# Sigmoid gates ahead of the latent attention, half of them parked in DRAM, and one output tile of the first branch per head

## The chip, the cores and the metric

The kernel runs on one core of a Trainium2 chip. The metric is device time in microseconds (us), from runs of the whole program; a profile is one more execution, recorded by the hardware. TensorE (PE) does the matrix products, with its weight loads as a row of their own (PEld); VectorE (DVE), ScalarE (ACT) and GpSimd (POOL) do the rest; SyncE (SP) issues the DMAs.

## The reference, cut to what matters

Two transformer blocks on 512 positions of width 1024, in float32. The change lies in the first half of the first block:

```
h = rms_norm(x, pre_mix_norm)
h_q, h_k, h_v, h_g, h_a, c_q, c_kv, k_pe = split(h @ w_in)
y_a = gla_branch(h_q, h_k, h_v, h_g, h_a, ...) @ w_o_gla          # first branch
y_b = mla_branch(c_q, c_kv, k_pe, cos, sin, ...) @ w_o_mla        # latent attention, 8 heads
g_a, g_b = split(sigmoid(h @ w_gate + b_gate))
mixed = (g_a * y_a + g_b * y_b) @ w_out
```

The latent attention normalises c_q and c_kv, makes from them the queries and keys of eight heads (128 columns without position and 64 with rope), and for blocks of 128 queries computes a masked softmax over the keys and its product with the values.

## The kernel before

**Layout.** Activations lie transposed: a tile has 128 features on the partitions and the 512 positions along the free side, so h is 8 tiles, the gates are 16 tiles (0 to 7 for the first branch, 8 to 15 for the second), and every output of width 1024 is 8 tiles. Each float32 operand is split into a high and a low part in a format that TensorE takes at full rate (`hi_lo`, line 129: ScalarE's cast at L135, VectorE's difference at L139 or L141). A product is three matmuls per step, high x high, low x high and high x low (`mm3`, line 205).

**A dense tile.** `lin` (line 212) makes one output tile of 128 x 512: it takes one of the PSUM banks of the ring `mm`, loads 512 KB of weights by one DMA on SP (`wload`, L179) into one of three raw buffers, splits them (two halves, L135 and L139), and runs 8 steps of 3 matmuls. `evac` (line 459) evicts the bank times the norm's factor R (L462 or L464). A gate is such a tile with a tanh after it (`gate`, lines 793 to 796); the sigmoid is written as half of one plus that tanh.

**Memory.** SBUF is cut by hand into 84 slots of 128 x 512 and 14 half slots; `A(name)` takes the slot that has been free longest and `free` puts it back at the end. A tile whose slot is still in use waits for it.

**Order.** The program is written as one long sequence, and a scheduler at build time fixes each engine's order: at each moment of a simulated timeline it takes, on every engine, the instruction earliest in the program among those whose inputs, slot and bank are ready. On the chip each engine then runs its list in that order, and so does SP with its DMAs. A DMA waits on SP for its buffer and its source. So later work can be placed ahead in gaps, but only as the simulated timeline saw them.

**The stages around the change.**

1. The first norm (lines 621 to 642). For the 8 tiles of x: the pair of x times the gain (ScalarE and VectorE), the weights of the first two output tiles, and their matmuls. Then, for each x, its square (ScalarE, L348) and the sum over the tiles (VectorE, L361). `hold2` holds two instructions behind which the squares and the sums are kept: here the last pair made. The sums give R through a small product (L375), a power on GpSimd (L332) and transposes (L383).
2. The first branch: its keys, values and queries, the scan over chunks in two halves of two heads (`gla_scan`), and its gated outputs (`gla_out`). The 8 tiles of its result (pairs, 16 slots) are `ogs`.
3. Lines 798 to 805. For n = 0 to 7: gate n, then output tile n of the first branch (`w_o_gla`), then `mix[n]` = (tanh + 1) x tile (L802). Then gates 8 to 11.
4. The latent attention's first inputs (lines 906 to 913): norms of c_q and c_kv, `mla_pair(0)` (rope queries of two heads and their values: rope copies on ScalarE at L613 and L614, two rows stacked by DMA at L851) and `mla_qk(0)`, `mla_qk(1)` (query and key of one head).
5. The loop over heads (lines 915 to 928). Head hd: its scores and softmax (`mla_scores`, L815 to L820, L887, L888), then the values of the head before it (`mla_values`, with transposes at L829), then the rope pair of heads hd + 2 and hd + 3 for even hd, and the query and key of head hd + 2. In heads 4 to 7 one more gate each, 12 to 15. After the last gate h and R are freed.
6. Lines 948 to 955. For n = 0 to 7: output tile n of the second branch (`w_o_mla`), times gate 8 + n, plus `mix[n]`. Then x is loaded again and the block goes on with `w_out`.

Of the kernel before, what the change touches and what calls it, by code (L numbers as in the profile page):

```python
# [10 lines left out]
F32 = mybir.dt.float32  # L11
# [3 lines left out]
ALU = mybir.AluOpType  # L15
AX = mybir.AxisListType

P = 128
T = 512
NT = T // P  # L20
DM = 1024
KD = DM // P
# [36 lines left out]
def two_blocks(ctx: ExitStack, tc: tile.TileContext, d, dbg=None):  # L59
    nc = tc.nc  # L60
    V, S, G, PE = nc.vector, nc.scalar, nc.gpsimd, nc.tensor

    NSLOT, NHALF = 84, 14
    cst = ctx.enter_context(tc.tile_pool(name="cst", bufs=1))
    ar = ctx.enter_context(tc.tile_pool(name="ar", bufs=1))
    pp = ctx.enter_context(tc.tile_pool(name="pp", bufs=1, space=bass.MemoryType.PSUM))


# [6 lines left out]
    def A(name, dt=F32, cols=T):  # L75
        if cols > 256 or len(spare_half) < 3:
            i = spare.popleft()
            low[0] = min(low[0], len(spare))
            ap = ar.tile([P, T], dt, tag="slot%d" % i, name=name)[:, :cols]
            owner[id(ap)] = (spare, i, ap, name)  # L80
        else:
            i = spare_half.popleft()
            ap = ar.tile([P, 256], dt, tag="half%d" % i, name=name)[:, :cols]
            owner[id(ap)] = (spare_half, i, ap, name)
        return ap

    def free(*xs):
        for x in xs:
            if isinstance(x, (tuple, list)):
                free(*x)  # L90
            else:
                home, i = owner.pop(id(x))[:2]
                home.append(i)
# [13 lines left out]
    def share(**kw):  # L107

        for name, which in kw.items():
            rings[name] = deque(which)  # L110

    def bank(name):
        i = rings[name].popleft()
        rings[name].append(i)
        return banks[i]

    MM, AT, OP, ST = (lambda: bank("mm")), (lambda: bank("at")), (lambda: bank("op")), (lambda: bank("st"))
# [26 lines left out]
    made, hold, hold2 = [], [], []  # L144
# [3 lines left out]
    def pair(name, src, scale=None, cols=T, eh=None, el=None):  # L148
        hi, lo = A(name + "h", F32R, cols), A(name + "l", F32R, cols)
        made[:] = hi_lo(hi[:, :cols], lo[:, :cols], src, scale, eh, el)  # L150
        return hi, lo
# [7 lines left out]
    def order(later, earlier):  # L159
        tc.add_manual_dep(later, earlier.name,  # L160
                          mybir.DependencyInfo(mybir.DependencyClass.NoSync, mybir.DependencyReason.DATA),
                          reason="table of functions")
# [27 lines left out]
    def wtile(w, n, kt, k0=0):  # L190

        step = 8
        ws = []
        for c0 in range(0, kt, step):
            ws.append(wload(w[n, :, (k0 + c0) * P:(k0 + min(kt, c0 + step)) * P]))
        return step, ws

    def wpart(wt, k):

        step, ws = wt  # L200
        hi, lo = ws[k // step][k % step // 4]
        s = slice(k % step % 4 * P, (k % step % 4 + 1) * P)
        return hi[:, s], lo[:, s]

    def mm3(ps, a, b, first, last):
        (ah, al), (bh, bl) = a, b
        r = PE.matmul(ps, lhsT=ah, rhs=bh, start=first, stop=False)  # L207
        PE.matmul(ps, lhsT=ah, rhs=bl, start=False, stop=False)  # L208
        PE.matmul(ps, lhsT=al, rhs=bh, start=False, stop=last)  # L209
        return r.ins  # L210

    def lin(w, n, hs, cols=T, k0=0, after=None):

        kt = len(hs)
        ps = MM()
        wt = wtile(w, n, kt, k0)
        for k in range(kt):
            r = mm3(ps[:, :cols], wpart(wt, k), hs[k], k == 0, k == kt - 1)
            if k == 0 and after:
                order(r, after)  # L220
        free(wt[1])
        return ps
# [178 lines left out]
    xs = [A("x") for k in range(KD)]  # L401
# [27 lines left out]
    def vcol(name, i=0, n=1):  # L429
        return vec[:, VOFF[name] + i:VOFF[name] + i + n]  # L430
# [16 lines left out]
    def normed(src_tiles, gain, n, before=None, **kw):  # L447

        st = Stat(n, **kw)
        hs = []  # L450
        for k, x in enumerate(src_tiles):
            if before:
                before(k)
            hs.append(pair("h", x, vcol(gain, k)))
        for x in src_tiles:
            st.add(x)
        return hs, st
# [9 lines left out]
    def repair(x, cols=T, eh=None, el=None):  # L467

        p = pair("pr", x[:, :cols], None, cols, eh, el)
        free(x)  # L470
        return p
# [147 lines left out]


    st = Stat(DM, esq=S, eadd=V)
    hs, pss, wps = [], [MM(), MM()], []
    for k, x in enumerate(xs):
        hs.append(pair("h", x, vcol("pre_mix", k)))
        last = list(made)
        if k in (0, 2, 4):
            c = PARTS[k // 2]
            wps.append([pair("w", raw[:, c], None, c.stop - c.start) for raw in w01])
            last = list(made)
        s_ = slice(k * P - PARTS[min(k // 2, 2)].start, (k + 1) * P - PARTS[min(k // 2, 2)].start)  # L630
        for ps, (wh, wl) in zip(pss, wps[-1]):
            mm3(ps, (wh[:, s_], wl[:, s_]), hs[k], k == 0, k == KD - 1)

    hold2[:] = last
    for x in xs:
        st.add(x)
    hold2[:] = []
    free(wps)
# [1 line left out]
    R, rt = st.done()  # L640
# [13 lines left out]
    for t in range(NT):  # L654
        q = slice(t * P, (t + 1) * P)
        ps = AT()
# [45 lines left out]
    for t, ps in enumerate(lin_tok(d["w1K"], 0, hs)):  # L702
        x = A("kdx")
# [83 lines left out]
    ogs = gla_out(0, ot0)  # L787
# [5 lines left out]
    def gate(n):  # L793
        z = evac(lin(d["w_gate"], n, hs), "gate", R)
        act("exp_tanh", z, z, AF.Tanh, scale=0.5, bias=half_bg[:, n:n + 1])
        return z

    mix = []
    for n in range(KD):
        g = gate(n)  # L800
        ps = lin(d["w_o_gla"], n, ogs)
        V.scalar_tensor_tensor(g, g, 1.0, ps, ALU.add, ALU.mult)  # L802
        mix.append(g)
    free(ogs)
    gbs = [gate(8 + n) for n in range(4)]


    share(mm=(0, 1, 2, 3), at=(4, 5, 6), op=(7,), st=(4, 5, 6))
    table_exp = ["exp_tanh"]

    def softmax(ps, w, mask):
# [50 lines left out]
    def mla_pair(hp):  # L862
        x = evac(lin(d["w_uq"], 8 + hp, cqs), "qpe", Rq, mscale)
        rope(x)
        xp = repair(x)
        Q2 = [stacked(xp, hh) for hh in range(2)]
        free(xp)
        vb = []
        for t, ps in enumerate(lin_tok_half(d["w_ukvV"], hp // 2, ckvs, hp % 2)):
            v = A("v", F32R)  # L870
            hi_lo(v[:, 0:256], v[:, 256:512], ps[:, 0:256], rkv[:, t:t + 1])
            vb.append(v)
        return Q2, vb

    def mla_qk(hd):
        qn = repair(evac(lin(d["w_uq"], hd, cqs), "qn", Rq, mscale))
        kn = repair(evac(lin(d["w_ukvK"], hd, ckvs), "kn", Rkv))
        return qn, kn
# [14 lines left out]
    def mla_values(pt, vb, hh):  # L893
# [9 lines left out]
            free(vb)  # L903
        return pair("om", op)

    cqs, stq = normed(cq, "q_norm", 384, esq=S, eadd=V)
    free(cq)
    Rq, _ = stq.done()
    ckvs, stkv = normed(ckv, "kv_norm", 256, esq=S, eadd=V)
    free(ckv)  # L910
    Rkv, rkv = stkv.done()
    oms = []
    pairs, qks = [mla_pair(0)], [mla_qk(0), mla_qk(1)]
    last = None
    for hd in range(8):
        Q2, vb = pairs[hd // 2]
        cur = (mla_scores(Q2[hd % 2], *qks[hd]), vb, hd % 2)
        if last:
            oms.append(mla_values(*last))
        last = cur  # L920
        if hd % 2 == 0 and hd < 6:
            pairs.append(mla_pair(hd // 2 + 1))
        if hd < 6:
            qks.append(mla_qk(hd + 2))
        if hd >= 4 and len(gbs) < KD:
            gbs.append(gate(8 + len(gbs)))
            if len(gbs) == KD:
                free(hs, R)
    oms.append(mla_values(*last))
    share_w[0] = 0  # L930
    free(cqs, ckvs, Rq, Rkv, K2a, K2b, cosT, sinT)
# [14 lines left out]


    ms = []
    for n in range(KD):
        g = gbs[n]  # L950
        ps = lin(d["w_o_mla"], n, oms)
        V.scalar_tensor_tensor(g, g, 1.0, ps, ALU.add, ALU.mult)
        V.tensor_tensor(g, g, mix[n], ALU.add)
        ms.append(pair("mx", g, 0.5))
        free(g, mix[n])
# [14 lines left out]
    xs = [A("x") for k in range(KD)]  # L970
# [21 lines left out]
    hs, sth = chained(xs, "pre_ffn", DM, post_norm(fs, st, "post_mix", xs))  # L992
# [11 lines left out]
    R = sth.R  # L1004
# [57 lines left out]
    for n in range(G1, KF, 2):  # L1062
# [4 lines left out]
        else:  # L1067
            for j, g in enumerate(zg):
                act("silu", g, g, AF.Silu)
                ps = lin(d["w_fgu"], 2 * (n + j) + 1, ns)  # L1070
                V.tensor_tensor(g, g, ps, ALU.mult)
                hid.append(repair(g))
        if n + 2 == G2:
            for m in range(KD):
                ps = lin(d["w_fd"], m, hid, k0=G1)
# [24 lines left out]
    hs, sth = chained(xs, "attn_norm", DM, post_norm(fs, st, "post_ffn", xs))  # L1100
# [45 lines left out]
    R = sth.R  # L1146
# [11 lines left out]
    ps = MM()  # L1158
# [154 lines left out]
    last, o = None, None  # L1313
    for hd in range(8):
# [6 lines left out]
        if hd % 2 == 0:  # L1321
            o = A("fo")
# [6 lines left out]
        last = (hd, pt, o)  # L1329
# [23 lines left out]
    last, o = None, None  # L1353
    for hd in range(9):
# [16 lines left out]
        if hd % 2 == 0:  # L1371
            o = A("so")
        if hd % 2 == 0 and hd < 6:
            sin_.append(sb_inputs(*sraw[hd // 2 + 1]))
        last = (hd, lks, q2, kst, o)
# [20 lines left out]
    hs, sth = chained(xs, "xattn", DM)  # L1396
# [8 lines left out]
    R = sth.R  # L1405
# [65 lines left out]
    hs, sth = chained(xs, "ffn_norm", DM)  # L1471
# [4 lines left out]
    R = sth.R  # L1476
# [205 lines left out]
```

## Time and profile before

| | us |
|---|---|
| median of 3 runs | 1749.28 |
| lowest and highest run | 1744.3, 1750.36 |
| the profiled execution | 1748.82 |
| its span, first to last instruction | 1747.0 |
| ScalarE, busy in the span | 886.7 |
| HBM read, written (MB) | 151.64, 2.10 |

The profile shows one execution. Its page has the busy time of each engine; a table by stretches gives the same for any part of the span, with the clock that TensorE was granted (1.00 is full speed) and the mean busy share of the 16 DMA engines. The list of waits says which instruction waited for which, in total, how often, and the longest. In a timeline a row is a start, a duration, the engine, the line and the operation; in brackets stands the idle time before it and what ended it. Matmuls overlap: the distance between two starts is what one costs, and it is shorter than the duration in its row. Near 190 to 320 us lie the gates and output tiles of the first branch, from about 320 to 480 the latent attention with its inputs, and then the second branch's output.

### The profile page before, as it was taken

What the parts mean: (1) busy time and instruction counts of PE and PEld (TensorE: products, weight loads), DVE (VectorE), ACT (ScalarE), POOL (GpSimd) and SP (SyncE); (2) the same over time, 40 slices, a digit from 0 to 9 for tenths busy, and PEclk for the clock granted to TensorE, in tenths of its full rate; (3) what the DMA queues carried; (4) which work ended last, traced back from release to release, by engine and by line L of the source; (5) the groups of instructions that cost most, each with busy time, mean ns of one, the idle gap of its engine ahead of it and who ended that gap; (6) DMA issues with size and microseconds to landing.
All of it is one profiled execution on the core that took longest, in us unless ns stands there. A gap on an engine that the chain in (4) does not pass through costs nothing.

```text
span 1747.0 us, 25844 instructions
## 1 busy us (share of the span) xinstructions
PE 1708.8 (98%) x9706; PEld 1490.0 (85%) x9706; DVE 1200.6 (69%) x2390; ACT 886.7 (51%) x1821; POOL 90.2 (5%) x109
## 2 busy tenths in 40 slices
PE   9999999999999999999999999999999999999998
PEld 7888888877889889989998888887998988988987
DVE  7547864587576866847777656787856598974863
ACT  6534443465544544424445666687525354652653
POOL 1000000100003100000013000000210200000000
PEclk9999999999999999999999999999999999999999
DMA  6212251123350322332333354433414123232321
GB/s 225 85 49 73 73 169 44 49 73 102 126 181 13 89 81 85 121 108 75 121 122 93 101 133 105 125 97 109 133 40 140 40 82 100 80 126 85 99 95 49
DMA packets 61646, 170.10 MB, mean 97 GB/s; under 512 B 7825, under 2 KB 13137, under 8 KB 61521
## 3 DMA queue, kind: packets, MB, share of 16 engines
q1 hardware_dynamic: 61104, 168.24, 31.6%
q8 instruction: 76, 1.25, 0.3%
q14 instruction: 50, 0.40, 0.1%
q10 hardware_dynamic: 288, 0.14, 0.0%
q0 software_dynamic: 128, 0.07, 0.0%
HBM read 151.64 MB, written 2.10 MB: 88 GB/s over the span
## 4 chain that ended last, share of the span: by engine, by line
PE 84%; DVE 7%; ACT 4%; DMA 2%; issue 2%; POOL 1%; SPq 0%; POOLq 0%; DVEq 0%; ACTq 0%
PE bank L207 26%; PE bank L209 26%; PE bank L208 26%; DVE wl L139 1%; PE bank L1235 1%; PE bank L829 1%; DVE hl L141 1%; ACT wh L135 1%; DVE f L961 1%; DMA wr<-w1K 1%; DMA wr<-w_mq 0%; PE bank L1195 0%; PE bank L1194 0%; POOL sq L361 0%; DVE prl L139 0%
## 5 line engine op out<-in xcount | busy, mean ns | idle before, releaser
L135 ACT CAST wh<-wr 128x512 fp32r<-128x512 f32 (+1 forms) x534 | 310.1, 605 | 377.7 <-PE bank L208 133.5
L139 DVE TENSOR_TENSOR wl<-wr,wh 128x512 fp32r<-128x512 f32 (+2 forms) x534 | 349.1, 672 | 169.6 <-ACT wh L135 141.2
L207 PE MATMUL bank<-hh,wh 128*128 128x512 f32 (+1 forms) x868 | 306.9, 356 | 6.0 <-ACT wh L135 4.2
L209 PE MATMUL bank<-hh,wl 128*128 128x512 f32 (+1 forms) x868 | 305.8, 353 | 0.0
L208 PE MATMUL bank<-hl,wh 128*128 128x512 f32 (+1 forms) x868 | 305.7, 353 | 0.1
L208 PE MATMUL bank<-prl,wh 128*128 128x256 f32 (+1 forms) x760 | 252.9, 333 | 0.0
L209 PE MATMUL bank<-prh,wl 128*128 128x256 f32 (+1 forms) x760 | 252.9, 333 | 0.0
L207 PE MATMUL bank<-prh,wh 128*128 128x256 f32 (+1 forms) x760 | 250.8, 334 | 0.6 <-ACT prh L135 0.6
L207 PEld LDWEIGHTS bank<-hh,wh 128*128 128x128 f32 x868 | 164.3, 190 | 28.2 <-ACT wh L135 5.6
L209 PEld LDWEIGHTS bank<-hh,wl 128*128 128x128 f32 x868 | 164.5, 190 | 22.3 <-DVE wl L139 1.3
L208 PEld LDWEIGHTS bank<-hl,wh 128*128 128x128 f32 x868 | 164.6, 190 | 21.4 <-DVE hl L141 1.3
L207 PEld LDWEIGHTS bank<-prh,wh 128*128 128x128 f32 x760 | 144.2, 190 | 14.9 <-ACT prh L135 1.0
L209 PEld LDWEIGHTS bank<-prh,wl 128*128 128x128 f32 x760 | 144.3, 190 | 14.4 <-DVE wl L139 0.4
L208 PEld LDWEIGHTS bank<-prl,wh 128*128 128x128 f32 x760 | 144.3, 190 | 14.1
L208 PE MATMUL bank<-nl,wh 128*128 128x512 f32 (+1 forms) x440 | 148.4, 337 | 0.0
L207 PE MATMUL bank<-nh,wh 128*128 128x512 f32 (+1 forms) x440 | 148.3, 337 | 0.0
L209 PE MATMUL bank<-nh,wl 128*128 128x512 f32 (+1 forms) x440 | 147.9, 337 | 0.0
L207 PEld LDWEIGHTS bank<-nh,wh 128*128 128x128 f32 x440 | 83.5, 190 | 8.9
L208 PEld LDWEIGHTS bank<-nl,wh 128*128 128x128 f32 x440 | 83.5, 190 | 8.8
L209 PEld LDWEIGHTS bank<-nh,wl 128*128 128x128 f32 x440 | 83.5, 190 | 8.9
L332 POOL TENSOR_TENSOR rtok<-sm,minus_half 128x2 f32<-128x2 f32 (+1 forms) x20 | 16.7, 835 | 1270.8 <-DVE sm L331 1270.8
L135 ACT CAST wh<-s 128x512 fp32r<-128x512 f32 x72 | 43.8, 620 | 67.8 <-DVE s L296 39.9
(400 smaller groups left out, 3366.8 us busy)
## 6 DMA issues: line engine op xcount, KB each, us to landing
wr<-w_up SPq DMA_DIRECT2D x38, 512.0 KB, 3.6
wr<-w_fgu SPq DMA_DIRECT2D x32, 512.0 KB, 3.7
wr<-w1T SPq DMA_DIRECT2D x16, 512.0 KB, 3.6
wr<-w_gate SPq DMA_DIRECT2D x16, 512.0 KB, 4.0
wr<-w_fd SPq DMA_DIRECT2D x16, 512.0 KB, 3.8
wr<-w2T SPq DMA_DIRECT2D x16, 512.0 KB, 3.8
wr<-w_dn SPq DMA_DIRECT2D x16, 512.0 KB, 3.7
wr<-w1K SPq DMA_DIRECT2D x12, 512.0 KB, 4.3
```

The lines of the kernel that those rows point to most:

```text
L135: r = S.copy(hi, src) if eh is S else V.tensor_copy(hi, src)
L139: q = el.tensor_tensor(lo, src, f(hi), ALU.subtract)
L141: q = V.scalar_tensor_tensor(lo, src, scale, f(hi), ALU.mult, ALU.subtract)
L207: r = PE.matmul(ps, lhsT=ah, rhs=bh, start=first, stop=False)
L208: PE.matmul(ps, lhsT=ah, rhs=bl, start=False, stop=False)
L209: PE.matmul(ps, lhsT=al, rhs=bh, start=False, stop=last)
L332: G.tensor_tensor(y, v, minus_half[:, :y.shape[1]], ALU.pow)
L829: PE.transpose(tp[:, i * P:(i + 1) * P], ps_tiles[i][:, b * P:(b + 1) * P], C("ident"))
L961: r = V.scalar_tensor_tensor(fs[k][:, c], fs[k][:, c], vcol(gain, k), st.R[:, c], ALU.mult, ALU.mult)
L1235: PE.matmul(z[:, (b2 - b) * P:w], lhsT=lt, rhs=part[:, :T - b2 * P], start=False, stop=False)
```

## The change

There are four parts. The squares of the first norm are each kept behind the pair two tiles further on (`marks[k + 2]`) in place of the last one. All 16 gates stand ahead of the heads: 8 to 15 right after the first branch, each copied to a DRAM tile by a DMA on SP and its slot freed; 0 to 7 between the norms and the first inputs of the latent attention, kept in SBUF. Each head then has one output tile of the first branch (`mix_a`), between the values of the head before and the next inputs. Ahead of the second branch's output the eight parked gates are loaded back. The sharing of the PSUM banks for the attention is set a little earlier, with the same banks for dense tiles.

```diff
+    dr = ctx.enter_context(tc.tile_pool(name="dr", bufs=1, space=bass.MemoryType.DRAM))
...
-    hs, pss, wps = [], [MM(), MM()], []
+    hs, pss, wps, marks = [], [MM(), MM()], [], []
     for k, x in enumerate(xs):
         hs.append(pair("h", x, vcol("pre_mix", k)))
-        last = list(made)
+        marks.append(list(made))
         if k in (0, 2, 4):
             c = PARTS[k // 2]
             wps.append([pair("w", raw[:, c], None, c.stop - c.start) for raw in w01])
-            last = list(made)
...
-    hold2[:] = last
-    for x in xs:
+    for k, x in enumerate(xs):
+        hold2[:] = marks[min(k + 2, KD - 1)]
         st.add(x)
...
-    mix = []
+
+    share(mm=(0, 1, 2, 3), at=(4, 5, 6), op=(7,), st=(4, 5, 6))
+
+    away = []
     for n in range(KD):
-        g = gate(n)
-        ps = lin(d["w_o_gla"], n, ogs)
-        V.scalar_tensor_tensor(g, g, 1.0, ps, ALU.add, ALU.mult)
-        mix.append(g)
-    free(ogs)
-    gbs = [gate(8 + n) for n in range(4)]
-
-
-    share(mm=(0, 1, 2, 3), at=(4, 5, 6), op=(7,), st=(4, 5, 6))
+        g = gate(KD + n)
+        o = dr.tile([P, T], F32, name="away%d" % n)
+        nc.sync.dma_start(o, g)
+        away.append(o)
+        free(g)
...
+    mix = [gate(0)]
     cqs, stq = normed(cq, "q_norm", 384, esq=S, eadd=V)
     free(cq)
     Rq, _ = stq.done()
+    mix.append(gate(1))
     ckvs, stkv = normed(ckv, "kv_norm", 256, esq=S, eadd=V)
     free(ckv)
     Rkv, rkv = stkv.done()
+    mix.append(gate(2))
+    pairs = [mla_pair(0)]
+    mix += [gate(n) for n in (3, 4)]
+    qks = [mla_qk(0)]
+    mix += [gate(n) for n in (5, 6)]
+    qks.append(mla_qk(1))
+    mix.append(gate(7))
+    free(hs, R)
+
+    def mix_a(n):
+        ps = lin(d["w_o_gla"], n, ogs)
+        V.scalar_tensor_tensor(mix[n], mix[n], 1.0, ps, ALU.add, ALU.mult)
+
     oms = []
-    pairs, qks = [mla_pair(0)], [mla_qk(0), mla_qk(1)]
     last = None
     for hd in range(8):
...
         last = cur
+        mix_a(hd)
         if hd % 2 == 0 and hd < 6:
             pairs.append(mla_pair(hd // 2 + 1))
         if hd < 6:
             qks.append(mla_qk(hd + 2))
-        if hd >= 4 and len(gbs) < KD:
-            gbs.append(gate(8 + len(gbs)))
-            if len(gbs) == KD:
-                free(hs, R)
+    free(ogs)
     oms.append(mla_values(*last))
...
     ms = []
+    gbs = [A("gate") for n in range(KD)]
+    for n in range(KD):
+        nc.sync.dma_start(gbs[n], away[n])
```

## The prediction

> **What bounds the kernel now.** I read the page first, then the table by stretches round the changed stages, then the waits inside the one bad stretch, then the timelines of single engines.
>
> ```profile
> span 1747.0 us, 25844 instructions
> PE 1708.8 (98%) x9706; PEld 1490.0 (85%) x9706; DVE 1200.6 (69%) x2390; ACT 886.7 (51%) x1821; POOL 90.2 (5%) x109
> ```
>
> TensorE bounds the whole. The change neither adds nor drops a matmul, so it can win only what TensorE loses: 38.2 us idle (1747.0 - 1708.8) and stretches at a low clock. The table (stretch, length, then busy time of each engine, granted clock, DMA share and GB/s) says where that lies around the latent attention:
>
> ```profile
> 320.00:340.00 20.00, 20.00 (x114) 17.51 (x113) 10.23 (x19) 9.77 (x18) 3.79 (x3) 1.00 0.13 36
> 340.00:360.00 20.00, 18.96 (x108) 16.04 (x108) 19.40 (x56) 14.24 (x36) 1.30 (x1) 1.00 0.37 96
> 360.00:380.00 20.00, 16.27 (x90) 14.49 (x89) 15.81 (x43) 12.50 (x31) 1.77 (x1) 0.83 0.24 60
> 380.00:400.00 20.00, 20.00 (x117) 17.46 (x116) 17.92 (x47) 13.57 (x33) 0.00 (x0) 1.00 0.16 46
> 400.00:420.00 20.00, 16.34 (x87) 13.90 (x87) 14.97 (x38) 10.94 (x27) 1.30 (x1) 0.91 0.55 145
> 420.00:440.00 20.00, 20.00 (x104) 17.16 (x103) 14.57 (x37) 11.03 (x26) 0.00 (x0) 1.00 0.26 79
> 440.00:460.00 20.00, 20.00 (x107) 17.11 (x107) 12.06 (x32) 12.31 (x26) 0.00 (x0) 1.00 0.25 80
> 460.00:480.00 20.00, 20.00 (x98) 16.82 (x97) 9.38 (x17) 8.21 (x18) 0.00 (x0) 1.00 0.51 185
> ```
>
> Up to 340 (gates 8 to 11 as cover) and from 420 (gates 12 to 15 as cover) TensorE is full. Between them it idles 1.04 + 3.73 + 3.66 = 8.4 us, and the clock rows take 0.17 x 20 = 3.4 us and 0.09 x 20 = 1.8 us more: 13.6 us visibly lost, all in the heads that have no tile of a dense product beside them. Two stalls make most of it:
>
> ```profile
> PE bank L207 <- ACT wh L135: 3.5, 1, 3.5
> PE bank L207 <- ACT pth L135: 1.9, 1, 1.9
> PE bank L208 <- DVE ptl L139: 1.8, 1, 1.8
> ACT wh L135 <- DMA wr<-w_gate: 3.3, 1, 3.3
> ```
>
> The second and third rows are one stall: the next matmul in TensorE's order needs a transposed block of softmax, and ScalarE's queue has four rope copies in front:
>
> ```profile
> 365.80 0.62 ACT L613 COPY rot<-qpe 32x512 f32<-32x512 f32 x1
> 367.69 0.61 ACT L614 COPY rot<-qpe 32x512 f32<-32x512 f32 x1
> 370.00:372.00 2.00, 0.50 (x1) 0.19 (x1) 2.00 (x5) 1.98 (x7) 0.16 (x1) 0.85 0.01 4
> 372.00:374.00 2.00, 1.64 (x5) 1.36 (x6) 2.00 (x6) 0.54 (x2) 0.00 (x0) 0.50 0.40 89
> 374.00:376.00 2.00, 2.00 (x10) 2.00 (x10) 1.55 (x5) 0.78 (x2) 0.00 (x0) 0.50 0.72 156
> 376.00:378.00 2.00, 2.00 (x11) 2.00 (x11) 0.70 (x5) 0.49 (x2) 0.00 (x0) 0.50 0.64 181
> ```
>
> Idle of 1.9 and 1.8 us is followed by a clock of 0.50 until 378 with TensorE full again. So a stall costs its idle time and about as much again. The other stall is a weight tile that came late:
>
> ```profile
> 404.74 0.80 SPq L406 DMA_DIRECT2D x<-xT  x2
> 405.64 0.38 SPq L179 DMA_DIRECT2D wr<-w_gate  x1
> 412.38 0.62 ACT L135 CAST wh<-wr 128x512 fp32r<-128x512 f32 x1 [3.33 <-DMA wr<-w_gate]
> 412.00:414.00 2.00, 0.00 (x0) 0.00 (x0) 0.97 (x2) 1.23 (x3) 0.00 (x0) 1.00 1.03 209
> ```
>
> Gate 12 is the first cover tile. Its 512 KB were issued only at 405.64, behind two tiles of x, with the DMA engines full (share 1.03); ScalarE waited 3.3 us for it and TensorE 3.5.
>
> The skill weighed against the first stall: the Trainium skill, "TensorE: Matmul & The Clock Gate", section "HAM oscillation — how this bites in real kernels", has as its rule that an idle gap over about 3.4 us brings the clock to half. Neither gap is that long, so by that rule the clock would have stayed up, only idle time could be won there, and the forecast below would be 3.4 us higher, 1739.6. The rows show 0.50 after gaps of 1.9 and 1.8 us; the measurement decides, and the sum goes by it.
>
> **The change, part by part.** One dense tile of eight steps is 24 matmuls:
>
> ```profile
> 300.02 0.39 PE L209 MATMUL bank<-prh,wl 128*128 128x512 f32 x1
> 300.24 0.39 PE L207 MATMUL bank<-prh,wh 128*128 128x512 f32 x1
> L462 DVE TENSOR_TENSOR gate<-bank,R x16: 681/691/693, 221.4 to 455.9; 128x512 f32<-128x512 f32 x16
> L802 DVE SCALAR_TENSOR_TENSOR gate<-gate,bank x8: 679/681/687, 236.8 to 302.5; 128x512 f32<-128x512 f32 x8
> L139 DVE TENSOR_TENSOR wl<-wr,wh 128x512 fp32r<-128x512 f32 (+2 forms) x534 | 349.1, 672 | 169.6 <-ACT wh L135 141.2
> ```
>
> Starts are 0.22 to 0.23 us apart, so a tile is 24 x 0.227 = 5.4 us of TensorE, whichever of the 16 gates or 8 output tiles it is. Moved, not changed: all 24 tiles, with their evictions (0.69), tanh and products (0.68).
>
> *One output tile per head.* Heads 0 to 5 each get 5.4 us of work whose inputs (the first branch's outputs and the finished gate) have long been there, so it needs only its weights. This is the cover that the good rows have. It also costs VectorE two subtractions (0.67) and the product: 2.0 us a head. Over 340 to 420 VectorE is busy 19.40 + 15.81 + 17.92 + 14.97 = 68.1 of 80 us. That stretch holds about six heads' scores (estimate, from their order in the program and the 24 softmax minima there); six tiles add 12.2 us of VectorE and 32.6 us of TensorE, and with the 13.6 us gone VectorE has 80.3 of 99 us, 81% against 85% now. It does not become the bound. The first stall goes because TensorE's order then has dense steps between the blocks; the second because weights for cover come once a head, from head 0 on, not as a first load at head 4. Heads 6 and 7 have two tiles where before four gates were left for the end; the second branch's output tiles can start on seven of their eight steps before the last head is done, so I count nothing there. What is late next is the same kind of wait, shorter. The rows with cover (380 to 400, 420 to 480) show 0 lost; ScalarE's rope copies stay, three more times, so I leave 2 us: between 0 and the 3.7 us that the first stall idles. Gain 13.6 - 2 = 11.6 us.
>
> *Gates 8 to 15 first, gates 0 to 7 among the first inputs.* The norms, rope and first heads' inputs had four gates (21.8 us) as cover and TensorE was full to 340; now they have eight. Nothing lost, nothing to win. The gates need only h, as gate 0 did; up to about 2 us of small waits in the first branch's second half could be filled, which no row of idle time shows: I take 0.
>
> *Parking.* Eight writes and eight reads of 256 KB on SP's queue.
>
> ```profile
> outT<-o SPq DMA_DIRECT2D x8, 256.0 KB, 2.4
> x<-xT SPq DMA_DIRECT2D x16, 256.0 KB, 4.0
> wr<-w_gate SPq DMA_DIRECT2D x16, 512.0 KB, 4.0
> 243.38 19.84 SPq L179 DMA_DIRECT2D wr<-w_gate  x5
> 318.80 0.69 DVE L462 TENSOR_TENSOR gate<-bank,R 128x512 f32<-128x512 f32 x1 [3.86 <-PE bank L209]
> ```
>
> The nearest write is the output's (2.4 us), the nearest read x (4.0). A write waits on SP for its tanh, and every weight load behind it waits too. But the last gate loads went out between 243 and 263 and the last of their gates was evicted at 318.8: SP runs tens of us ahead, so this is covered; uncovered, it is the third rival. The reads stand ahead of the second branch's weights and of x. As x went out at 404.74, long before its use after 540, they will go out early and have several tiles' time. 4.2 MB at the 209 GB/s of the full row is 20 us of DMA over some 200 us where the share is 0.13 to 0.55: hidden, except when a burst meets a weight tile as at 412 (second stall, 5.4 us with its clock), the first rival.
>
> *Squares of the first norm.* They no longer wait for all eight pairs.
>
> ```profile
> 14.03 4.26 ACT L348 ACTIVATE sq<-x 128x512 f32<-128x512 f32 x8
> 18.85 0.50 PE L207 MATMUL bank<-hh,wh 128*128 128x512 f32 x1 [0.61 <-ACT wh L135]
> 37.50 0.65 PE L383 MATMUL bank<-con,rtok 128*128 128x128 f32 x4 [0.77 <-POOL rtok L332]
> 39.42 1.16 PE L599 MATMUL bank<-rope_w,sel 128*128 128x128 f32 x8 [0.38 <-ACT R L389]
> ```
>
> Two or three of the eight squares (0.53 each) can go into ScalarE's waits for x. TensorE's waits that hang on this are 0.61 + 0.77 + 0.38 = 1.8 us. Against it, squares among the last pairs delay those by at most a few times 0.53 us, which TensorE would see for 0.5 us at most. Bounds +0.5 to -1.8; I take -1.0, since the first wait goes straight away and the later two depend on the order in VectorE's queue.
>
> **Sum.** The profiled execution took 1748.8 us (span 1747.0 and 1.8 around it), 0.5 below the median 1749.28, so it stands for the runs. 1748.8 - 11.6 - 1.0 = 1736.2. About 0.5% (8.7 us) is what a measurement of this kernel can tell from no change: the line is 1740.1.
>
> **The rivals.** (1) *One stall stays or comes back.* The order of instructions on each engine is fixed by a simulated timeline; where the chip runs later than that (rope on ScalarE, a burst of parked gates or x on the DMA engines), cover stands a few instructions away from the hole. For it: the stall at 370 had other heads' inputs as cover too and still came. Against: 380 to 400 is full with VectorE at 17.92 of 20. It gives back 5.4 to 7.1 us: 1741.6 to 1743.3. Chance 0.25.
> (2) *Nothing is won.* The stalls come from in-order queues alone and return in other heads, and the first norm gains 0: 1747 to 1749. Against it speak the three full rows from 420 on. Chance 0.08.
> (3) *Parking plugs SP: slower.* If weight loads stand directly behind a write, the next tile's weights start 1.4 us after a gate's last matmul (0.69 eviction and as much for tanh), land 4.0 us later and need 1.3 us of split: 6.7 us against 5.4 us of the tile between. With two tiles of lead nothing is lost; with one, 8 x 1.3 = 10 us, which takes the gain back (1746.6); with none, 8 x 6.7 = 54 us and 1790, with half of the gates so 1763. It decides where the lead falls below one tile, with most slots taken: by my count of the program 71 of 84 at gate 7. Against it is the lead of the rows at 243. Chance 0.07 for slower.
> The Trainium skill, "DMA: Bandwidth & Descriptors", section "Anatomy of one DMA — SWDGE (gpsimd) path", speaks for rival 3: a wait sits on the issuing sequencer, and completion is slowest when the target is HBM. The trace doesn't bear the second half out: the output's writes land in 2.4 us, x in 4.0.
>
> **How the numbers follow.** The forecast, 1730 to 1740, has 0.60: its ends are all visible loss gone plus the full 1.8 at the start and a few hidden us, and 5 us left in place of 2. Rival 1 has 0.25, rival 2 0.08, rival 3 0.07. The range runs from 1728 to 1747, through rivals 1 and part of 2. Faster: 0.60 and a little of rival 1, 0.62. Same: 0.31. Slower: 0.07.
>
> **What would show it.** Right: over the heads, stretches of 20 us with TensorE at 20.00 and clock 1.00, the wait for a transposed block and for gate weights gone, one output tile between any two heads' scores. The parked reads should land long before the first product that uses them. Wrong: a stretch with clock under 0.95 among the heads, the split (L135) waiting for a weight or parked tile by DMA, or SP's own waits on a tanh with TensorE idle behind it. At the start the squares should begin before 14 us and the wait at 18.85 be gone.

## The result and the profile after

The changed kernel takes 1736.19 us (median of 6 runs, 1734.4 to 1737.85) against 1749.03 for the kernel before (6 runs), a ratio of 0.9932 with a 95% interval of 0.9918 to 0.9947: 12.8 us less, where 12.6 had been worked out. The sum came out. Its terms did not: in the runs below a step that the prediction had at nothing is by itself worth more than half of the gain.

The profiled execution took 1737.63 us. Its page:

```profile
span 1735.8 us, 25856 instructions
PE 1703.2 (98%) x9706; PEld 1487.2 (86%) x9706; DVE 1197.7 (69%) x2390; ACT 885.5 (51%) x1821; POOL 92.5 (5%) x109
```

The helper lines have moved by one (L207 is now L208, and so on). The table by stretches of the kernel after, with the same columns as before (busy time of PE, PEld, DVE, ACT and POOL, granted clock, DMA share, GB/s):

```profile
320.00:340.00 20.00, 20.00 (x109) 17.33 (x108) 13.45 (x38) 11.65 (x27) 1.75 (x1) 1.00 0.21 57
340.00:360.00 20.00, 20.00 (x106) 16.93 (x105) 15.28 (x40) 9.63 (x23) 0.00 (x0) 1.00 0.24 66
360.00:380.00 20.00, 20.00 (x119) 17.51 (x118) 16.54 (x43) 14.22 (x34) 1.80 (x1) 1.00 0.39 111
380.00:400.00 20.00, 20.00 (x111) 17.33 (x109) 12.57 (x33) 9.77 (x23) 0.00 (x0) 1.00 0.15 45
400.00:420.00 20.00, 20.00 (x111) 17.03 (x110) 17.21 (x45) 11.28 (x29) 1.80 (x1) 1.00 0.53 155
420.00:440.00 20.00, 20.00 (x111) 17.40 (x111) 14.66 (x43) 12.10 (x28) 0.00 (x0) 1.00 0.41 117
440.00:460.00 20.00, 20.00 (x100) 16.85 (x99) 10.07 (x19) 8.09 (x19) 0.00 (x0) 1.00 0.56 199
460.00:480.00 20.00, 18.58 (x86) 15.28 (x85) 15.80 (x26) 10.59 (x19) 0.00 (x0) 1.00 0.49 162
```

TensorE is full at full clock through all eight heads, where it had idled 8.4 us and run twice at a low clock. One wait is left up to 480 us, 1.4 us near 469, in the second branch's output.

For the runs below one instruction serves as a milestone: the first matmul of the squares' sum of the first block's mixed output. Everything changed lies ahead of it. In the timeline of TensorE it stands, before and after, in these rows:

```profile
539.40 0.61 PE L375 MATMUL bank<-con,sq 128*128 128x2 f32 x4 [0.93 <-DVE sq L361]
```

```profile
527.28 0.61 PE L376 MATMUL bank<-con,sq 128*128 128x2 f32 x4 [0.94 <-DVE sq L362]
```

12.1 us are won there. The rest of the span is 1207.6 us before (1747.0 - 539.4) and 1208.5 after.

### The profile page after: what moved, and what is told of

It reads as the page before. It is cut to its first block, busy times and chain, and to the rows that moved or that the text cites. A ratio compares the mean times of both kernels' runs of the same rounds, so it can differ in the third digit from the quotient of the medians.

```text
span 1735.8 us, 25856 instructions
## 1 busy us (share of the span) xinstructions
PE 1703.2 (98%) x9706; PEld 1487.2 (86%) x9706; DVE 1197.7 (69%) x2390; ACT 885.5 (51%) x1821; POOL 92.5 (5%) x109
## 4 chain that ended last, share of the span: by engine, by line
PE 84%; DVE 7%; ACT 3%; DMA 3%; issue 2%; POOL 1%; POOLq 0%; DVEq 0%; ACTq 0%
PE bank L208 26%; PE bank L210 26%; PE bank L209 26%; DVE wl L140 1%; DMA wr<-w_o_mla 1%; PE bank L1250 1%; DVE hl L142 1%; ACT wh L136 1%; PE bank L828 1%; DVE f L976 1%; DMA wr<-w_mq 1%; DVE sq L362 1%; DMA wr<-w1K 0%; PE bank L1209 0%; PE bank L1210 0%
## 5 line engine op out<-in xcount | busy, mean ns | idle before, releaser
L136 ACT CAST wh<-wr 128x512 fp32r<-128x512 f32 (+2 forms) x534 | 310.7, 605 | 364.4 <-PE bank L209 122.1
L140 DVE TENSOR_TENSOR wl<-wr,wh 128x512 fp32r<-128x512 f32 (+1 forms) x534 | 349.8, 673 | 167.1 <-ACT wh L136 145.8
L208 PE MATMUL bank<-hh,wh 128*128 128x512 f32 (+1 forms) x868 | 306.2, 355 | 1.9 <-DVE z L1016 1.7
L208 PE MATMUL bank<-prh,wh 128*128 128x256 f32 (+1 forms) x760 | 251.3, 334 | 0.6 <-ACT prh L136 0.6
L208 PEld LDWEIGHTS bank<-hh,wh 128*128 128x128 f32 x868 | 164.6, 190 | 23.0 <-ACT hh L138 1.9
L208 PEld LDWEIGHTS bank<-prh,wh 128*128 128x128 f32 x760 | 144.3, 190 | 15.0 <-ACT prh L136 1.0
L208 PE MATMUL bank<-nh,wh 128*128 128x512 f32 (+1 forms) x440 | 148.3, 337 | 0.0
L208 PEld LDWEIGHTS bank<-nh,wh 128*128 128x128 f32 x440 | 83.5, 190 | 9.0
L333 POOL TENSOR_TENSOR rtok<-sm,minus_half 128x2 f32<-128x2 f32 (+1 forms) x20 | 17.5, 877 | 1203.0 <-DVE sm L332 1203.0
```

The source lines that it names most:

```text
L136: r = S.copy(hi, src) if eh is S else V.tensor_copy(hi, src)
L140: q = el.tensor_tensor(lo, src, f(hi), ALU.subtract)
L333: G.tensor_tensor(y, v, minus_half[:, :y.shape[1]], ALU.pow)
```

## The experiments

Each kernel was run at least five times beside the kernel before, and its ratio is to the runs of before beside it (medians 1748.08 to 1748.43 us; the 1749.03 in the table stands beside the changed kernel). "Milestone" is the start of the matmul above in the run's profile, "rest" its span less that. Both are read from a single execution. after, no_squares, park_twice and r_by_vector have the same stages in the same places from the first branch on, and their milestones spread over 1.2 us, so smaller differences than that are not read as effects.

| run | median us | ratio to before, 95% interval | milestone | rest |
|---|---|---|---|---|
| before | 1749.03 | 1 | 539.40 | 1207.6 |
| squares_only | 1748.38 | 0.9999, 0.9989 to 1.0009 | 539.61 | 1207.9 |
| gates_ahead | 1745.14 | 0.9986, 0.9977 to 0.9995 | 534.78 | 1210.8 |
| gates_early | 1744.1 | 0.9977, 0.9967 to 0.9986 | 533.10 | 1211.0 |
| gates_between | 1739.5 | 0.9949, 0.9935 to 0.9962 | 531.95 | 1207.6 |
| no_cover | 1740.74 | 0.9955, 0.9942 to 0.9969 | 530.63 | 1208.8 |
| late_cover | 1737.99 | 0.9943, 0.9930 to 0.9955 | 526.62 | 1209.0 |
| after | 1736.19 | 0.9932, 0.9918 to 0.9947 | 527.28 | 1208.5 |
| no_squares | 1736.62 | 0.9934, 0.9922 to 0.9947 | 526.69 | 1208.5 |
| no_park | 1738.29 | 0.9945, 0.9932 to 0.9957 | 526.62 | 1210.7 |
| park_twice | 1735.73 | 0.9931, 0.9918 to 0.9945 | 526.80 | 1208.1 |
| r_by_vector | 1737.56 | 0.9934, 0.9922 to 0.9947 | 527.88 | 1208.2 |
| best_park | 1736.56 | 0.9934, 0.9921 to 0.9946 | 526.09 | 1208.4 |
| best_no_park | 1737.51 | 0.9943, 0.9930 to 0.9955 | 529.75 | 1206.0 |

### The squares alone, and the change without them

squares_only is the kernel before with this edit; no_squares is the changed kernel with it undone.

```diff
-    hold2[:] = last
-    for x in xs:
+    for k, x in enumerate(xs):
+        hold2[:] = marks[min(k + 2, KD - 1)]
         st.add(x)
```

Expected of squares_only:

> The kernel before with the first part of the change alone: the squares of the first norm each behind the pair two tiles on. Theory (all of the gain comes from cover in the heads, since R is copied by ScalarE behind a weight cast that waits for its DMA): nothing to 0.5 us either way, about 1749, and R's copy still starts near 39 us though the sums are ready about 3.5 us earlier. Rival (the forecast's own term): 1.0 us faster, 1748, with R's copy at 38 or before. No head is touched, so both stalls (near 370 and 413 us) stay at their 3.7 and 3.5 us.

Expected of no_squares:

> The changed kernel with the squares of the first norm held back as before. Theory (the squares won nothing): within 1 us of the changed kernel, 1735 to 1737.5, the first evictions of the first branch's keys near 71.4 us as in the kernel before. Rival (the forecast's term): 1 us or more slower than the changed kernel, 1737 or over, with those evictions later than 72.

Both times came out as the theory had it: 0.9999 for the squares alone, 0.9934 without them against 0.9932 with them. The reason stands in the timelines of VectorE (first row) and of ScalarE, kernel after:

```profile
32.24 0.15 DVE L332 TENSOR_SCALAR sm<-bank 128x4 f32<-128x4 f32 x1
...
36.77 0.62 ACT L136 CAST wh<-wr 128x512 fp32r<-128x512 f32 x1 [2.24 <-DMA wr<-w1K]
...
37.72 1.28 ACT L167 ACT_TABLE_LOAD   x1
39.02 0.59 ACT L390 COPY R<-bank 128x512 f32<-128x512 f32 x1
```

The sums are read at 32.24, 3.6 us earlier than before (35.80). But a later step of R, its copy on ScalarE, stands in that engine's queue behind a weight cast that waits for its DMA and behind a table load: 39.02 now, 38.78 before. A chain was shortened whose end waits for something else.

### R copied by VectorE

```diff
-            S.copy(self.R[:, c], pb[:, :w])
+            (V.tensor_copy if self.on_v else S.copy)(self.R[:, c], pb[:, :w])
```

with `on_v` set for the first norm of the changed kernel alone.

> The changed kernel with the first norm's R copied from PSUM by VectorE in place of ScalarE. Theory (the squares won nothing because R's copy stood on ScalarE behind a weight cast waiting for its DMA and a table load): R is copied near 37.5 us, 1.5 us sooner, the waits of TensorE near 38 to 40 us shrink and 1 to 1.5 us are won: 1734.5 to 1735.5, and the first evictions of the first branch's keys start 1 us or more ahead of 71.6. Rival (something else, the weight tile's DMA itself, holds TensorE there): 1736, evictions at 71.6.

VectorE's timeline in that run:

```profile
36.80 0.69 DVE L390 COPY R<-bank 128x512 f32<-128x512 f32 x1 [1.71 <-PE bank L384]
```

R comes 2.2 us sooner and the first eviction of the first branch's keys 1.4 us (70.26 against 71.63), so R's copy on ScalarE was what held them. The whole time did not fall (1737.56 us, 0.9934, where 1734.5 to 1735.5 had been expected): the milestone is at 527.88, 0.6 us later than in the changed kernel, though this kernel still led by 1.3 at 212 us. The heads are as full as in the changed kernel. The lead goes in the second branch's output, at the wait that the changed kernel has there too:

```profile
468.90 0.50 PE L208 MATMUL bank<-omh,wh 128*128 128x512 f32 x1 [1.80 <-DVE gate L968]
470.00:472.00 2.00, 2.00 (x7) 1.51 (x6) 2.00 (x5) 0.69 (x2) 0.00 (x0) 0.51 0.50 195
472.00:474.00 2.00, 2.00 (x7) 1.63 (x6) 2.00 (x4) 1.48 (x3) 0.00 (x0) 0.63 0.29 72
```

It is 1.80 us in place of 1.42, and behind it the granted clock falls to 0.51 and 0.63 with TensorE full, which costs 0.49 x 2 + 0.37 x 2 = 1.7 us more. In the changed kernel the clock stayed at 1.00 there.

### All gates ahead, and the first inputs among them

Both runs start from the kernel before. The output tiles stay ahead of the heads, no head has a dense tile, nothing is parked. In gates_ahead gates 12 to 15 only join 8 to 11:

```diff
-    gbs = [gate(8 + n) for n in range(4)]
+    gbs = [gate(8 + n) for n in range(KD)]
+    free(hs, R)
...
-        if hd >= 4 and len(gbs) < KD:
-            gbs.append(gate(8 + len(gbs)))
...
```

> The kernel before with one edit: gates 12 to 15 follow gates 8 to 11, ahead of the attention's first inputs; no head has a dense tile, nothing is parked. The run without cover took 7.4 us off, so cover is not all of it. Theory now: the stall near 413 was the late load of gate 12 and goes with it; the stall near 370 comes from the first inputs, made right ahead of head 0, which crowd VectorE and ScalarE in the first heads, and stays: 1742 to 1746, clock under 0.95 once in the first heads. Rival (both stalls were want of cover): 1749 to 1755. Rival (it is enough that all gates are ahead): 1739 to 1741.

In gates_between the same eight gates stand one or two at a time between the norms, `mla_pair(0)`, `mla_qk(0)` and `mla_qk(1)`, as gates 0 to 7 do in the changed kernel:

```diff
+    gbs = [gate(8)]
     cqs, stq = normed(cq, "q_norm", 384, esq=S, eadd=V)
...
+    gbs.append(gate(10))
+    pairs = [mla_pair(0)]
+    gbs += [gate(n) for n in (11, 12)]
+    qks = [mla_qk(0)]
+    gbs += [gate(n) for n in (13, 14)]
+    qks.append(mla_qk(1))
+    gbs.append(gate(15))
...
```

> The kernel before with gates 8 to 15 among the attention's first inputs (one after each step, as gates 0 to 7 are in the changed kernel) and the output tiles left ahead of the heads: no cover, nothing parked, squares as before. Theory: first inputs are ready a gate or two before head 0, so neither stall comes: 1739 to 1742, as in the run without cover. Rival (the place of the first inputs does not matter): the same time as the run with all gates ahead of the inputs, within 1.5 us.

Two stretches of gates_ahead in its first heads, and its longest waits of TensorE:

```profile
380.00:400.00 20.00, 17.18 (x91) 15.20 (x91) 16.11 (x43) 12.89 (x32) 1.78 (x1) 0.83 0.21 53
400.00:420.00 20.00, 20.00 (x126) 17.97 (x125) 18.19 (x52) 15.43 (x39) 1.81 (x1) 1.00 0.22 69
```

```profile
PE bank L208 <- DVE ptl L139: 1.6, 2, 1.4
PE bank L207 <- ACT pth L135: 1.5, 1, 1.5
```

The second stall of the kernel before, the late weights of gate 12, is gone with its load: 4.6 us at the milestone. The first stall is there with the same two waits and the same drop of the clock. In gates_between:

```profile
380.00:400.00 20.00, 19.69 (x123) 17.72 (x122) 18.51 (x51) 14.47 (x37) 1.81 (x1) 1.00 0.23 60
400.00:420.00 20.00, 18.22 (x106) 15.54 (x105) 18.49 (x52) 15.20 (x37) 1.80 (x1) 0.96 0.40 121
420.00:440.00 20.00, 19.71 (x112) 16.81 (x110) 16.68 (x51) 11.21 (x30) 0.00 (x0) 0.96 0.22 60
```

One wait of 1.5 us is left of the pair, with still no dense tile beside any head, and it too is followed by a low clock (0.96 in two stretches):

```profile
417.07 0.50 PE L207 MATMUL bank<-pth,v 128*128 128x512 f32 x1 [1.48 <-ACT pth L135]
418.00:420.00 2.00, 2.00 (x6) 1.58 (x7) 2.00 (x5) 1.33 (x4) 0.00 (x0) 0.55 0.92 260
```

Idle time and clock together take 2.82 + 3.4 = 6.2 us in the stalled stretch of gates_ahead, and 1.78 + 0.29 + 1.6 = 3.7 from 400 to 440 here. The milestone is 2.8 us earlier. So the place of the first inputs alone takes some 2.5 of the 6.2 us away. The ratios, 0.9949 against 0.9986, lie further apart, but more than half of that difference is in the rest, which is 3.2 us shorter here though nothing in it was edited. In gates_between the first inputs are evicted from 324 to 355 us and the first scores follow at 361; in the kernel before they were evicted from 331 to 342, the next pair's among them, and the scores began at 343. That the scheduler's order for the following heads then has more room is how I read it; which instruction's place decides was not tried by itself.

### The change without cover, and with cover late

no_cover is the changed kernel with all eight output tiles ahead of the heads; late_cover has two in each of heads 4 to 7:

```diff
+    for n in range(KD):
+        mix_a(n)
+    free(ogs)
...
     for hd in range(8):
...
-        mix_a(hd)
...
```

```diff
-        mix_a(hd)
+        if hd >= 4:
+            mix_a(2 * hd - 8)
+            mix_a(2 * hd - 7)
```

Expected of no_cover, the first of the two to run:

> The changed kernel with its eight output tiles of the first branch all ahead of the heads, none between them; gates, parking and squares as changed. Theory: all eight heads are without cover, so at least the 13.6 us visibly lost before come back and heads 4 to 7 add some: 1749 to 1756, with TensorE idle and a clock under 0.95 in the heads. Rival (gates ahead or squares make the gain): 1735 to 1739.

Expected of late_cover:

> The changed kernel with the eight output tiles as two per head in heads 4 to 7, none in heads 0 to 3. Theory (cover is worth some 4 us over eight heads, a wait here and there in each): 1737 to 1740, between the changed kernel and the run without cover, the waits of heads 0 to 3 back and those at the last head gone. Rival (cover decides in the first heads, where both stalls of the kernel before were): 1744 to 1750.

no_cover broke the theory that the prediction had. It takes 1740.74 us, 0.9955, where the return of both stalls and 1749 to 1756 had been expected; the rival's 1735 to 1739 is nearer, though it is missed too. Its heads:

```profile
360.00:380.00 20.00, 20.00 (x117) 17.62 (x117) 16.71 (x51) 13.81 (x35) 1.81 (x1) 1.00 0.29 76
380.00:400.00 20.00, 19.66 (x119) 17.26 (x118) 18.20 (x45) 13.05 (x31) 1.29 (x1) 1.00 0.21 54
400.00:420.00 20.00, 18.51 (x114) 15.95 (x113) 18.61 (x55) 15.65 (x40) 1.80 (x1) 1.00 0.43 117
420.00:440.00 20.00, 19.78 (x116) 16.98 (x115) 18.31 (x56) 13.78 (x36) 0.00 (x0) 1.00 0.49 156
440.00:460.00 20.00, 20.00 (x110) 17.33 (x110) 12.58 (x34) 10.97 (x24) 0.00 (x0) 1.00 0.50 154
460.00:480.00 20.00, 18.48 (x87) 14.87 (x86) 14.20 (x25) 9.94 (x19) 0.00 (x0) 1.00 0.52 176
```

Eight heads in a row without cover lose 2.1 us in their middle and 1.5 at the end, and the clock never falls, although VectorE is busy 18.2 to 18.6 of 20 us. Cover then takes 3.35 us more off at the milestone (530.63 to 527.28); by the medians it is 4.5 us, by the ratios 4.0, with intervals that overlap a little. In late_cover the heads with tiles are full, and one of the others shows the old kind of wait:

```profile
340.00:360.00 20.00, 18.29 (x106) 15.62 (x105) 17.02 (x51) 13.32 (x36) 1.84 (x1) 1.00 0.33 96
360.00:380.00 20.00, 20.00 (x109) 17.02 (x108) 14.87 (x39) 11.01 (x28) 0.00 (x0) 1.00 0.15 45
```

That is 1.7 us in three waits, the longest 1.0 for the split of a block of softmax, yet its milestone, 526.62, is no later than with one tile per head: it has no wait near 469. Where the tiles stand among the heads is of no weight that these runs resolve, once inputs and gates are out of the way.

### Cover without the rest

gates_early is the kernel before with gates 12 to 15 in heads 0 to 3.

```diff
-        if hd >= 4 and len(gbs) < KD:
+        if hd < 4:
             gbs.append(gate(8 + len(gbs)))
```

> The kernel before with one edit: gates 12 to 15 stand in heads 0 to 3 in place of 4 to 7. Nothing is parked, the output tiles of the first branch stay ahead. Theory (a stall is a head without a dense tile beside it): the stalls near 370 and 413 go, and waits come in heads 4 to 7, which now have none, though heads 6 and 7 also have less to compute: 1739 to 1744. Rival (the stalls come from in-order queues whatever stands beside them): 1747 to 1750, with a clock under 0.95 in one of the first heads.

```profile
360.00:380.00 20.00, 20.00 (x107) 17.13 (x106) 14.21 (x35) 9.97 (x23) 0.00 (x0) 1.00 0.12 34
380.00:400.00 20.00, 18.77 (x105) 15.92 (x104) 16.02 (x43) 13.28 (x32) 1.79 (x1) 1.00 0.40 116
400.00:420.00 20.00, 20.00 (x117) 17.51 (x116) 14.59 (x38) 13.59 (x31) 0.07 (x1) 1.00 0.24 70
460.00:480.00 20.00, 18.00 (x89) 14.57 (x87) 13.65 (x25) 9.33 (x19) 0.00 (x0) 1.00 0.50 159
```

Both stalls go at their old size, the longest of TensorE's waits for the softmax is now 1.1 us, and the clock stays at 1.00. The last heads, now bare, lose 2.0 us from 460 to 480: 6.3 us are won at the milestone, of which 3.4 are given back in the rest, and the time, 1744.1 us, is at the far end of what had been expected. So a dense tile beside a head takes these stalls away by itself, as the prediction said, but with four gates in heads 0 to 3 it wins 6.3 us and not 11.6. Eight output tiles between the heads, with the other parts left as before, were not run. The two edits are two cures for the same stalls, 6.3 us and 7.4 us (gates_between) alone and 12.1 together, so they overlap in part.

### Parking: none, and twice

no_park keeps the eight gates in SBUF; park_twice writes each to two DRAM tiles and reads both back.

```diff
-        o = dr.tile([P, T], F32, name="away%d" % n)
-        nc.sync.dma_start(o, g)
-        away.append(o)
-        free(g)
+        away.append(g)
```

```diff
         nc.sync.dma_start(o, g)
+        o2 = dr.tile([P, T], F32, name="again%d" % n)
+        nc.sync.dma_start(o2, g)
...
+        nc.sync.dma_start(gbs[n], away[n][0])
+        nc.sync.dma_start(gbs[n], away[n][1])
```

Expected of no_park:

> The changed kernel with gates 8 to 15 kept in SBUF: no write to DRAM, no reading back; at most 79 of 84 slots are then taken ahead of the heads in place of 71. Theory (parking is hidden and the slots are enough): 1734 to 1737, the wait of 1.4 us near 469, where a weight tile of the second branch lands late among reads, gone. Rival (parking is what makes room for weights ahead): weights are split late near the last gates, ScalarE or VectorE waits for slots and TensorE for them, 1740 to 1746.

Expected of park_twice:

> The changed kernel with each parked gate written to two DRAM tiles and read back from both, one after the other, into the same slot: twice the traffic and twice the DMAs of parking. Theory (parking is hidden, but reading back shares the DMA engines with the second branch's weights): the first products of the second branch wait up to 2 us more near 469, 1736 to 1739. Rival (parking costs nothing at all): 1735 to 1737 and no longer wait there. Rival (writes hold up SP's queue): TensorE idle among the gates from 220 to 300 us, 1742 or more.

Milestones 526.62 without, 527.28 with, 526.80 with double parking: it costs nothing that these runs resolve. park_twice in the stretch that it loads most, and the one behind it:

```profile
440.00:460.00 20.00, 20.00 (x99) 16.88 (x98) 10.16 (x19) 8.13 (x18) 0.00 (x0) 1.00 0.79 278
460.00:480.00 20.00, 18.26 (x84) 15.02 (x83) 16.27 (x27) 10.79 (x19) 0.00 (x0) 1.00 0.48 158
```

With 278 GB/s in place of 199 TensorE's wait near 469 is 1.7 us in place of 1.4. That is no more than it varies with single parking and one tile per head (1.0 in no_squares, 1.8 in r_by_vector). Without parking the stretch from 460 to 480 is full (20.00), but so it is in late_cover, which parks, so parking alone does not make the wait. park_twice takes 1735.73 us, below the theory's range and inside the first rival's; the wait that this rival wanted gone is there. no_park takes 1738.29 us, between its theory and its rival. That is 2 us more in the median than the changed kernel, with intervals that overlap, and its rest is 2.2 us longer. Nothing in the rest was edited. Compared place by place in the traces, TensorE's order there differs from that of the kernel before in 152 of 7105 places. But this order does not settle the time of the rest: gates_ahead, gates_early and no_cover have one and the same order of TensorE behind the milestone, and rests of 1210.8, 1211.0 and 1208.8 us. The cause stays open.

### Putting the parts together

best_park joins late cover and R by VectorE; best_no_park drops the parking as well.

> The changed kernel with two output tiles per head in heads 4 to 7 and R copied by VectorE, the gates parked. Theory: statistics of the mixed output at 525 to 526.3, 1734 to 1737. Rival (the parts do not add): 526.5 or later, 1736.5 to 1740.

> The changed kernel without parking, with two output tiles per head in heads 4 to 7, and R copied by VectorE. Theory (each of the three won 0.7 to 1.4 us up to the statistics of the first block's mixed output, at 527.3 in the changed kernel): these start at 524.5 to 526, and the time is 1733 to 1736 unless the second block's order falls on its slow side (2 to 3 us more), as it did in two of the earlier runs. Rival (the three do not add, since each moves the order of the heads): statistics at 526.5 or later, 1736 to 1740.

best_park reaches the earliest milestone, 526.09, with TensorE full from 460 to 480, and 1736.56 us, both inside its theory's range; but late_cover alone is at 526.62, and the ratio (0.9934) can't be told from the changed kernel's. best_no_park lost 2.8 us of TensorE's time from 320 to 420 and had the shortest rest; its milestone, 529.75, is its rival's. So no run shows the parts adding, and no version here beats the changed kernel by more than its runs resolve.

## Why the prediction was right, and which step of it was wrong

*The sum, 1736.2 us.* Measured: 1736.19. That it agrees so closely is luck. The runs of the kernel after lie 3.5 us apart and those of before 6.1, the two profiled executions differ by 11.2 us and their milestones by 12.1, and a term that was far too large nearly cancelled one that had been put at nothing.

*The 13.6 us lost in the heads.* Right: they were there to win, and 12.1 are won at the milestone.

*"Nothing lost, nothing to win"* (gates 8 to 15 first, gates 0 to 7 among the first inputs). This step failed. Alone, without any cover, it is worth 7.4 us at the milestone: 4.6 with gates 12 to 15 ahead, where the late load of gate 12 no longer stands in a head, and 2.8 more with the first inputs ready a gate or more ahead of head 0. The prediction had looked only at whether TensorE was full up to 340, not at what the place of those inputs does to the heads behind.

*One output tile per head, 11.6 us.* As a term of the sum it was mis-sized: on top of the other part it is 3.35 us. Tried the other way round (gates_early, four gates as cover) it removes both stalls at their old size and wins 6.3 us, so its mechanism holds; the error was to give the whole gain to one of two cures that overlap.

*2 us left over.* 1.4 are left, but not of the kind named. It is a weight tile of the second branch that comes late (5.1 us from its issue at 462.19): VectorE waits in its queue with the split of that tile, and with it the eviction that frees TensorE's bank. That is rival 1's mechanism, smaller. Rows of SP, ScalarE, VectorE and TensorE:

```profile
462.19 0.33 SPq L180 DMA_DIRECT2D wr<-w_o_mla  x1
467.34 2.40 ACT L136 CAST wh<-wr 128x512 fp32r<-128x512 f32 x4 [0.57 <-DMA wr<-w_o_mla]
467.99 1.29 DVE L140 TENSOR_TENSOR wl<-wr,wh 128x512 fp32r<-128x512 f32 x2 [0.50 <-ACT wh L136]
469.20 0.68 DVE L967 SCALAR_TENSOR_TENSOR gate<-gate,bank 128x512 f32<-128x512 f32 x1
469.94 0.50 PE L208 MATMUL bank<-omh,wh 128*128 128x512 f32 x1 [1.42 <-DVE gate L967]
```

*Squares, -1.0 us.* Measured: nothing. The signs came: in the kernel after the squares begin at 9.46 us, and the waits at 18.85 and 37.50 are gone. But others took their place (0.84 at 20.57, for a weight split on VectorE), and the last one, behind R's copy, grew from 0.38 to 0.62 us. This last step hung on ScalarE's queue, not on VectorE's as the prediction had it, and its matmul starts at 39.66 where it had started at 39.42.

*Parking hidden.* Right. In the list of DMAs of the kernel after the writes land in 2.0 us and the reads in 4.8 (median of 8 each; 2.4 and 4.0 had been taken):

```profile
away<-gate SPq DMA_DIRECT2D x8, 256.0 KB, 2.0
gate<-away SPq DMA_DIRECT2D x8, 256.0 KB, 4.8
```

Rival 3's plug is real but covered. SP's own waits from 215 to 480:

```profile
SPq L805 <- ACT gate L171: 17.5, 6, 8.0
```

SP stood 17.5 us in all behind writes that waited for their tanh, once for 8.0 us, and TensorE missed none of it: weights were far enough ahead.

*Rival 2* is refuted by the full rows. Rival 1's two stalls are in none of the other runs near their old size, except the first in gates_ahead and both in squares_only, whose heads are those of the kernel before.

*The clock.* The Trainium skill, "TensorE: Matmul & The Clock Gate", section "HAM oscillation — how this bites in real kernels", warns of idle gaps over about 3.4 us. The runs show that shorter ones can suffice. gates_ahead has gaps of 1.5 and 1.4 us close together and then a clock of 0.83 over 20 us; in gates_between one of 1.48, with one of 0.29 right behind it, is followed by 0.55, and in r_by_vector a single one of 1.80 by 0.51. Others of that length leave the clock at 1.00: 1.42 us in the kernel after, 1.74 in park_twice. So the length of a gap does not settle it, and what does is not shown here. Counting half speed for the first stall, as the trace of before showed it, was right.

## What to carry to other kernels

When two edits attack the same stall, price each alone and then the second on top of the first, since their gains can overlap. Ask of a moved step what it does to the stage behind it, not only whether its own stage was full. And where a scheduler orders the whole program, read an edit at a milestone just behind it: here the part behind it moved by up to 5 us though nobody had edited it.

## What the runs showed that I had not expected

With the same instructions behind the milestone, the rest of the span lay between 1206.0 us (best_no_park) and 1211.0 (gates_early), a spread as large as many of the effects studied, and 2.2 us apart even with the same order of TensorE. And eight heads of attention, with VectorE busy over 18 of 20 us in their middle, ran without cover at a cost of 3.6 us (no_cover). That this is so because their inputs are ready when they start is my reading.
